# Feed-forward of a two-layer decoder trunk: a third column block by seven products in every second group, squares by ScalarE, first activations transposed by TensorE

## The chip, the core and the metric

The kernel runs on one core of a Trainium2 chip. A core has five engines with instruction streams of their own: TensorE (PE in the profile; its weight loads are PEld), VectorE (DVE), ScalarE (ACT), GpSimd (POOL) and SyncE (SP), which here only starts DMAs. Each takes its instructions in the order in which they stand and waits on semaphores. TensorE writes its products into PSUM, eight banks of 512 fp32 columns; the other engines copy them out. The metric is the device time of one execution, in microseconds, as the median of several runs.

## What is computed

Two layers, each a mixer and a dense feed-forward (FFN) with a squared ReLU. The change lies in the FFN, which runs once in each layer.

```python
# D_MODEL = 2048, SEQ = 256, DEPTH = 2, FFN_HIDDEN = 8192, all float32
def rmsnorm(x, w):
    y = x * lax.rsqrt(jnp.mean(jnp.square(x), axis=-1, keepdims=True) + EPS)
    return y * w

def squared_relu_mlp(h, w_up, w_down):
    return jnp.square(jax.nn.relu(h @ w_up)) @ w_down

def reference(x, ...):
    h = x                                   # (1, 256, 2048)
    for layer in range(DEPTH):              # 0: linear attention, 1: spatial gating
        y = mixer(rmsnorm(h, norm_w[layer, 0]), ...)
        h = h + rmsnorm(y, norm_w[layer, 1])
        y = squared_relu_mlp(rmsnorm(h, norm_w[layer, 2]), ffn_w_up[layer], ffn_w_down[layer])
        h = h + rmsnorm(y, norm_w[layer, 3])
    return h
```

## The kernel before

**Numbers.** Every fp32 product is made of three matmuls. `split` and `weights` divide an operand into a rounded part (hi, type fp32r, by ScalarE: lines 125 and 189) and the remainder (lo, by VectorE: lines 126 and 190); a product is x_hi·w_hi + x_lo·w_hi + x_hi·w_lo (lines 132 to 134, 318 to 320 and 362 to 364).

**Weights.** They come from HBM in tiles of 128 x 2048 fp32 (1 MB) over SP's queue into three buffers (`raw`), and are divided into four buffers of hi (`whi`) and four of lo (`wlo`). A buffer is used again when its last reader is done.

**The FFN.** `first_chunk` makes the first 512 of the 8192 hidden columns with tokens on the partitions (two halves of 128 tokens, b = 0 and 1). Its result must be turned round, hidden columns onto partitions: VectorE does that with 16 transposes of 32 x 32 blocks for each half (`blocks`, line 218). Then a loop runs over c = 1 to 15. A pass of it makes the next 512 hidden columns (`up_pass`, four quarters of 48 matmuls of 256 columns, PSUM tiles `tp`), and multiplies the 512 before them, group g = c - 1, with the down weights, in four blocks of 512 output columns (`block`), one behind each quarter: the order is `ORDER`, and in the first pass `FIRST`, where block 1 stands behind the second quarter, block 0 behind the third, and blocks 3 and 2 behind the fourth. `relu2` takes ReLU on ScalarE (line 386) and squares on GpSimd (line 387); the result is divided into the tiles e, and `sums` (lines 398 to 401) makes the sums f that seven-product blocks want. The last group is done by `down_last`, which also normalises.

**The blocks.** Blocks 0 and 2 (`SEVEN`) are made by seven products instead of eight: the 256 x 512 block is taken as 2 x 2 halves (Strassen's scheme in Winograd's form), `mul7` adds weights on VectorE (lines 341 to 343, tile `qsum`) and divides 1536 plain and 2048 summed columns, so that two `whi` and two `wlo` buffers are taken, and `chunk7` issues 42 matmuls of 256 columns into four PSUM tiles, two of the pool `acc` and two of `mx`, which VectorE adds to four accumulators (line 416). After the loop `combine` makes the two result tiles of a block from these (lines 441 to 447). Block 1 (`KEPT`) is made plainly by 24 matmuls of 512 columns that accumulate in two PSUM banks (`kept`) through all 15 groups; `acc_to_y` copies them after the last. Block 3 is made plainly, and copied or added to `y` in each group (lines 240 and 242). The pool `acc` has four banks, of which `kept` holds two; `mx` and `tp` have two each.

**Order.** The kernel is written in program order; a scheduler sets the order of each engine's instructions from it, with weight preparation and PSUM copies moved ahead or back, and that order is fixed when the program is built.

## Time and profile before

| | |
|---|---|
| median of three runs | 2547.78 us (2545.24 to 2547.9) |
| profiled execution: time / span | 2548.88 us / 2547.1 us |
| mean granted TensorE clock | 0.994 |
| TensorE, VectorE, ScalarE, GpSimd busy | 2506.0, 1968.8, 1201.2, 285.8 us |
| one pass in the middle of a FFN loop, from ReLU to ReLU | 43.69 us |
| in such a pass: TensorE, VectorE, ScalarE, GpSimd busy | 43.69, 37.00, 21.67, 2.58 us |
| GpSimd's squares (line 387) | 64, 83.0 us in all |
| VectorE's transposes of the first activations (line 218, from rl) | 64, 19.3 us in all |

The span runs from the first to the last instruction; the execution's time has 1.78 us around it. Busy shares are means over the program; matmuls are pipelined, so the time from the start of one to the start of the next says more than the duration that the profile gives to one. Idle time stands in brackets with the engine and line that ended it.

### The profile page before, as it was taken

To read this page: it belongs to the slowest core of one execution; us is meant where nothing else is said; L and a number is where in the kernel's file an instruction comes from. 1 tells how busy PE (TensorE), PEld (TensorE's weight loads), DVE (VectorE), ACT (ScalarE), POOL (GpSimd) and SP (SyncE) were. 2 spreads that over 40 slices of the span, in tenths; PEclk is the share of its full clock that TensorE was granted. 3 is DMA by queue.
4 is the path that set the end of the run, shared out by engine and by line. 5 is a ranking of instruction groups with operands and counts; after the bars stand their busy time and mean duration, and the time that the engine had idled before them with its cause. 6 is when DMAs were issued, how large, how long until landed. Compare 5 with 4: busy or idle time off the path is not lost.

```text
span 2547.1 us, 36465 instructions
## 1 busy us (share of the span) xinstructions
PE 2506.0 (98%) x15138; PEld 2211.3 (87%) x15138; DVE 1968.8 (77%) x2256; ACT 1201.2 (47%) x1174; POOL 285.8 (11%) x222
## 2 busy tenths in 40 slices
PE   8999999999999999999999999999999999999998
PEld 7778888878999999999878877777789999999997
DVE  7586855579888888888854596876898888888887
ACT  6555444454454454545544333333544544445453
POOL 3000201140000000000310110110400000000001
PEclk9999999999999999999999999999999999999999
DMA  6444544544555455555555455555445554555553
GB/s 245 181 151 147 187 162 175 204 155 174 195 195 199 183 204 192 190 192 205 204 204 194 170 203 202 190 202 199 149 165 199 189 206 185 198 192 189 191 201 139
DMA packets 81255, 478.04 MB, mean 188 GB/s; under 512 B 13633, under 2 KB 15809, under 8 KB 26817
## 3 DMA queue, kind: packets, MB, share of 16 engines
q1 hardware_dynamic: 81088, 475.70, 51.1%
q8 instruction: 119, 1.95, 0.3%
q14 instruction: 48, 0.39, 0.0%
HBM read 473.04 MB, written 2.62 MB: 187 GB/s over the span
## 4 chain that ended last, share of the span: by engine, by line
PE 45%; DVE 4%; POOL 1%; issue 1%; ACT 0%; DVEq 0%; POOLq 0%; ACTq 0%
PE acc L133 9%; PE acc L134 9%; PE acc L132 9%; PE tp L318 4%; PE tp L319 4%; PE tp L320 4%; PE acc L362 1%; PE acc L364 1%; PE acc L363 1%; DVE wlo L126 1%; PE mx L363 1%; PE mx L362 1%; PE mx L364 1%; DVE h L275 1%; DVE bc L218 1%
## 5 line engine op out<-in xcount | busy, mean ns | idle before, releaser
L126 DVE TENSOR_TENSOR wlo<-raw,whi 128x2048 fp32r<-128x2048 f32 (+3 forms) x380 | 860.3, 2267 | 269.1 <-ACT whi L125 267.1
L125 ACT ACTIVATE whi<-raw 128x2048 fp32r<-128x2048 f32 (+3 forms) x380 | 714.1, 1880 | 566.3 <-PE acc L133 319.2
L318 PE MATMUL tp<-xh,whi 128*128 128x256 f32 x1920 | 539.5, 281 | 0.0
L319 PE MATMUL tp<-xl,whi 128*128 128x256 f32 x1920 | 539.2, 281 | 0.0
L320 PE MATMUL tp<-xh,wlo 128*128 128x256 f32 x1920 | 538.9, 281 | 0.0
L132 PE MATMUL acc<-whi,xh 128*128 128x512 f32 (+3 forms) x1120 | 446.3, 398 | 5.8 <-ACT whi L125 5.8
L134 PE MATMUL acc<-wlo,xh 128*128 128x512 f32 (+3 forms) x1120 | 440.0, 393 | 5.1 <-DVE wlo L126 5.1
L133 PE MATMUL acc<-whi,xl 128*128 128x512 f32 (+3 forms) x1120 | 438.9, 392 | 0.0
L318 PEld LDWEIGHTS tp<-xh,whi 128*128 128x128 f32 x1920 | 361.5, 188 | 2.7
L319 PEld LDWEIGHTS tp<-xl,whi 128*128 128x128 f32 x1920 | 361.6, 188 | 2.5
L320 PEld LDWEIGHTS tp<-xh,wlo 128*128 128x128 f32 x1920 | 361.7, 188 | 0.0
L134 PEld LDWEIGHTS acc<-wlo,xh 128*128 128x128 f32 x1120 | 212.1, 189 | 53.2 <-DVE wlo L126 7.0
L132 PEld LDWEIGHTS acc<-whi,xh 128*128 128x128 f32 x1120 | 212.4, 190 | 51.8 <-ACT whi L125 6.3
L133 PEld LDWEIGHTS acc<-whi,xl 128*128 128x128 f32 x1120 | 212.3, 190 | 44.7 <-issue 1.0
L387 POOL TENSOR_TENSOR rl<-rl 128x512 f32<-128x512 f32 x64 | 83.0, 1313 | 1261.0 <-ACT rl L386 1136.3
L189 ACT ACTIVATE whi<-qsum 128x2048 fp32r<-128x2048 f32 x60 | 115.3, 1922 | 179.9 <-DVE qsum L343 178.9
L190 DVE TENSOR_TENSOR wlo<-qsum,whi 128x2048 fp32r<-128x2048 f32 x60 | 138.7, 2312 | 79.0 <-ACT whi L189 77.0
L416 DVE TENSOR_TENSOR y<-acc,y 128x512 f32<-128x512 f32 x112 | 76.9, 687 | 86.1 <-PE acc L364 86.1
L189 ACT ACTIVATE whi<-raw 128x1536 fp32r<-128x1536 f32 x60 | 89.6, 1493 | 108.2 <-DMA raw<-dn 79.0
L133 PE MATMUL acc<-whi,e1l 128*128 128x512 f32 x288 | 114.0, 396 | 0.0
L134 PE MATMUL acc<-wlo,e1h 128*128 128x512 f32 x288 | 113.8, 395 | 0.0
L132 PE MATMUL acc<-whi,e1h 128*128 128x512 f32 x288 | 113.7, 395 | 0.0
(350 smaller groups left out, 4212.8 us busy)
## 6 DMA issues: line engine op xcount, KB each, us to landing
raw<-up SPq DMA_DIRECT2D x128, 1024.0 KB, 4.8
raw<-dn SPq DMA_DIRECT2D x128, 1024.0 KB, 4.8
raw<-sg_in SPq DMA_DIRECT2D x64, 1024.0 KB, 4.8
raw<-la_in SPq DMA_DIRECT2D x56, 1024.0 KB, 4.8
raw<-sg_out SPq DMA_DIRECT2D x32, 1024.0 KB, 4.8
raw<-la_out SPq DMA_DIRECT2D x16, 1024.0 KB, 4.8
raw<-la_in SPq DMA_DIRECT2D x4, 768.0 KB, 4.4
kq<-xT SPq DMA_DIRECT2D x8, 256.0 KB, 6.1
```

The costliest lines, as they stand in the source:

```text
L125: ACT.activation(a, r, AF.Copy)
L126: V.tensor_tensor(d, r, a.bitcast(F32), ALU.subtract)
L132: PE.matmul(ps, xh, wh, start=first, stop=False)
L133: PE.matmul(ps, xl, wh, start=False, stop=False)
L134: PE.matmul(ps, xh, wl, start=False, stop=last)
L189: ACT.activation(hi, src, AF.Copy)
L190: V.tensor_tensor(lo, src, hi.bitcast(F32), ALU.subtract)
L318: PE.matmul(out, wh[:, col], xh, start=k == 0 and m % 2 == 0, stop=False, skip_group_check=True)
L319: PE.matmul(out, wh[:, col], xl, start=False, stop=False, skip_group_check=True)
L320: PE.matmul(out, wl[:, col], xh, start=False, stop=k == NKT - 1, skip_group_check=True)
L387: G.tensor_tensor(r, r, r, ALU.mult)
L416: V.tensor_tensor(Y[key], ps, Y[key], ALU.add)
```

## The change

Four things change, all in `ffn`; the line numbers of the mixers move by one.

1. `SEVEN` holds block 1 as well. In groups with an odd g (seven of the 15) block 1 goes through `chunk7` into accumulators of its own; in the eight with an even g it still accumulates in the two `kept` banks. These are no longer copied after the last group: `combine(1)` adds them from PSUM.
2. `relu2` squares on ScalarE (Square, in place) instead of GpSimd.
3. The first activations are transposed by TensorE, four transposes of 128 x 128 for each half into a PSUM tile of `mx`, which ScalarE copies to SBUF (tile `rl`). VectorE's 32 transposes of each FFN are gone.
4. The accumulators are allocated at the start of the FFN; two of the three of 256 columns share a tile.

```diff
--- before.py
+++ after.py
@@ -30,7 +30,7 @@
 PARTS = [4, 2, 1, 1]
 WAIT = [26, 30]
 AHEAD = 200
-SEVEN, KEPT = (0, 2), 1
+SEVEN, KEPT = (0, 1, 2), 1
 ORDER = (None, 0, None, 1, None, 2, None, 3)
 FIRST = (None, None, 1, None, 0, None, 3, 2)
 
@@ -384,7 +384,7 @@
             def relu2(ps):
                 r = T(fp, [P, 512], "rl", bufs=3)
                 ACT.activation(r, ps, AF.Relu)
-                G.tensor_tensor(r, r, r, ALU.mult)
+                ACT.activation(r, r, AF.Square)
                 return r
 
             def rows_in(tags):
@@ -408,28 +408,22 @@
 
             Y, kept = {}, [bank(acc, 512, "acc") for _ in range(2)]
 
-            def add(key, ps, first, n=512):
-                if first:
-                    Y[key] = T(hp, [P, 512], *BUF[key])[:, :n]
-                    V.tensor_copy(Y[key], ps)
-                else:
-                    V.tensor_tensor(Y[key], ps, Y[key], ALU.add)
-
-            BUF = {("a", 0): ("y00",), ("b", 0): ("y10",), ("a", 2): ("y02",), ("b", 2): ("y12",)}
+            half = T(hp, [P, 512], "bc", bufs=4)
+            Y.update({("d", 0): half[:, :256], ("d", 2): half[:, 256:], ("d", 1): T(fp, [P, 256], "d1")})
             for c in SEVEN:
-                BUF["c", c] = BUF["d", c] = ("bc", F32, 4)
+                Y["a", c], Y["b", c] = T(hp, [P, 512], f"y0{c}"), T(hp, [P, 512], f"y1{c}")
+                Y["c", c] = T(hp, [P, 512], "bc", bufs=4)
 
             def block(c, g, e, f):
 
-                if c in SEVEN:
-                    ps = chunk7(dn, fp, e, f, rows(g), c * 512)
-                    for k, p, n in zip("abcd", ps, (512, 512, 512, 256)):
-                        add((k, c), p, g == 0, n)
+                if c in SEVEN and not (c == KEPT and g % 2 == 0):
+                    for k, p in zip("abcd", chunk7(dn, fp, e, f, rows(g), c * 512)):
+                        if g == (c == KEPT):
+                            V.tensor_copy(Y[k, c], p)
+                        else:
+                            V.tensor_tensor(Y[k, c], p, Y[k, c], ALU.add)
                 elif c == KEPT:
                     chunk_tok(dn, kts([e]), rows(g), [(c * 512, 512)], 512, kept, g == 0, g == last - 1)
-                    if g == last - 1:
-                        for b in range(2):
-                            acc_to_y(kept[b], b, c, True)
                 else:
                     for b, p in enumerate(chunk_tok(dn, kts([e]), rows(g), [(c * 512, 512)], 512)):
                         acc_to_y(p, b, c, g == 0)
@@ -445,15 +439,22 @@
                 V.tensor_tensor(u, u, b[:, r], ALU.add)
                 V.tensor_tensor(b[:, l], u, p[:, r], ALU.add)
                 V.tensor_tensor(b[:, r], p[:, l], u, ALU.subtract)
+                if c == KEPT:
+                    V.tensor_tensor(a, kept[0], a, ALU.add)
+                    V.tensor_tensor(b, kept[1], b, ALU.add)
                 y[0][c], y[1][c] = a, b
 
             def halves_of(tiles):
                 return [[t[:, m] for m in range(2)] for t in tiles]
 
             e = pair("e0")
-            t = [T(hp, [P, 512], "bc", bufs=4) for _ in range(2)]
+            t = []
             for b, ps in first_chunk(up, X, [(0, 512)]):
-                blocks(t[b], relu2(ps))
+                r, tp = relu2(ps), bank(mxp, 512, "mx")
+                for j in range(4):
+                    PE.transpose(tp[:, j * P : (j + 1) * P], r[:, j * P : (j + 1) * P], ident)
+                t.append(T(fp, [P, 512], "rl", bufs=3))
+                ACT.activation(t[b], tp, AF.Copy)
                 sl = slice(b * P, (b + 1) * P)
                 split(e[0][:, :, sl], e[1][:, :, sl], t[b].rearrange("p (j c) -> p j c", c=P))
             v = [a.rearrange("p (i m t) -> p i m t", i=2, t=P) for a in t]
```

The scheduler moves other work with it. **First place: TensorE in the first pass, from block 3 to block 2** (`acc` of line 362 is block 2's first tile in PSUM, `mx` its others, `tp` the up products). Before, from the first product of block 2:

```order
L362 MATMUL mx_957_5179<-whi_952_5166,f0h_903_4787 128x256
L363 MATMUL mx_957_5179<-whi_952_5166,f0l_904_4788 128x256
L364 MATMUL mx_957_5179<-wlo_954_5168,f0h_903_4787 128x256
L362 MATMUL mx_957_5179<-whi_952_5166,f0h_903_4787 128x256
L363 MATMUL mx_957_5179<-whi_952_5166,f0l_904_4788 128x256
L364 MATMUL mx_957_5179<-wlo_954_5168,f0h_903_4787 128x256
L362 MATMUL mx_959_5181<-whi_953_5167,f0h_903_4787 128x256
L363 MATMUL mx_959_5181<-whi_953_5167,f0l_904_4788 128x256
L364 MATMUL mx_959_5181<-wlo_955_5169,f0h_903_4787 128x256
L362 MATMUL mx_959_5181<-whi_953_5167,f0h_903_4787 128x256
L362 MATMUL acc_956_5178<-whi_952_5166,e0h_882_4614 128x256
L363 MATMUL acc_956_5178<-whi_952_5166,e0l_883_4615 128x256
```

Changed, up to the first product of block 2 into `acc`:

```order
L363 MATMUL mx_968_5168<-whi_962_5154,e0l_894_4626 128x256
L364 MATMUL mx_968_5168<-wlo_964_5156,e0h_893_4625 128x256
L318 MATMUL tp_971_5217<-xh0_816_4336,whi_974_5220 128x256
L319 MATMUL tp_971_5217<-xl0_817_4337,whi_974_5220 128x256
L320 MATMUL tp_971_5217<-xh0_816_4336,wlo_975_5221 128x256
L318 MATMUL tp_971_5217<-xh0_816_4336,whi_974_5220 128x256
L319 MATMUL tp_971_5217<-xl0_817_4337,whi_974_5220 128x256
L320 MATMUL tp_971_5217<-xh0_816_4336,wlo_975_5221 128x256
L318 MATMUL tp_972_5218<-xh0_816_4336,whi_974_5220 128x256
L319 MATMUL tp_972_5218<-xl0_817_4337,whi_974_5220 128x256
L320 MATMUL tp_972_5218<-xh0_816_4336,wlo_975_5221 128x256
L362 MATMUL acc_965_5165<-whi_961_5153,e0h_893_4625 128x256
```

Ten products of block 2 into `mx` stood ahead of its first one into `acc`; now eighteen do, and nine up products of the next pass.

**Second place: VectorE in the same pass**, from the sums of the next pass's weights (line 341) to the copy of block 3 out of PSUM (line 240), by which block 2's first `acc` bank comes free. Before:

```order
L341 TENSOR_TENSOR qsum_972_5291<-raw_971_5290 128x1024
L400 TENSOR_TENSOR tr_940_5119<-rl_938_5109 128x256
L342 TENSOR_TENSOR qsum_972_5291<-qsum_972_5291,raw_971_5290 128x512
L343 TENSOR_TENSOR qsum_972_5291<-qsum_972_5291,raw_971_5290 128x512
L126 TENSOR_TENSOR wlo_970_5238<-raw_968_5236,whi_969_5237 128x2048
L190 TENSOR_TENSOR e1l_906_4792<-rl_938_5109,e1h_905_4791 128x512
L190 TENSOR_TENSOR e1l_906_4792<-rl_939_5112,e1h_905_4791 128x512
L398 TENSOR_TENSOR tr_940_5119<-rl_938_5109,rl_939_5112 128x256
L240 COPY y03_948_5160<-acc_943_5128 128x512
```

Changed:

```order
L341 TENSOR_TENSOR qsum_977_5274<-raw_976_5273 128x1024
L342 TENSOR_TENSOR qsum_977_5274<-qsum_977_5274,raw_976_5273 128x512
L400 TENSOR_TENSOR tr_949_5106<-rl_947_5096 128x256
L343 TENSOR_TENSOR qsum_977_5274<-qsum_977_5274,raw_976_5273 128x512
L190 TENSOR_TENSOR e1l_919_4783<-rl_947_5096,e1h_918_4782 128x512
L398 TENSOR_TENSOR tr_949_5106<-rl_947_5096,rl_948_5099 128x256
L399 TENSOR_TENSOR tr_949_5106<-tr_949_5106,rl_947_5096 128x256
L401 TENSOR_TENSOR tr_949_5106<-tr_949_5106,rl_948_5099 128x256
L126 TENSOR_TENSOR wlo_975_5221<-raw_973_5219,whi_974_5220 128x2048
L190 TENSOR_TENSOR e1l_919_4783<-rl_948_5099,e1h_918_4782 128x512
L190 TENSOR_TENSOR f1l_951_5112<-tr_949_5106,f1h_950_5111 128x1024
L240 COPY y03_957_5147<-acc_952_5115 128x512
```

The copy stood behind four instructions on the activations (400, 190, 190, 398) and now stands behind all seven, the division of the sums f among them.

**Third place: VectorE in an odd pass** (g = 3), around block 0's four additions to its accumulators (line 416 before, 424 changed; from two tiles `acc` and two `mx`). Before, where block 1 is plain, up to the sums of block 2's weights:

```order
L416 TENSOR_TENSOR y00_931_5047<-acc_1075_6166,y00_931_5047 128x512
L126 TENSOR_TENSOR wlo_1084_6272<-raw_1082_6270,whi_1083_6271 128x2048
L416 TENSOR_TENSOR y10_932_5049<-acc_1077_6168,y10_932_5049 128x512
L416 TENSOR_TENSOR bc_934_5053<-mx_1076_6167,bc_934_5053 128x256
L416 TENSOR_TENSOR bc_933_5051<-mx_1078_6169,bc_933_5051 128x512
L126 TENSOR_TENSOR wlo_1087_6302<-raw_1085_6300,whi_1086_6301 128x2048
L341 TENSOR_TENSOR qsum_1089_6355<-raw_1088_6354 128x1024
L190 TENSOR_TENSOR wlo_1092_6358<-raw_1088_6354,whi_1090_6356 128x1536
L342 TENSOR_TENSOR qsum_1089_6355<-qsum_1089_6355,raw_1088_6354 128x512
```

Changed, from the sums of block 1's weights to those of block 2's:

```order
L341 TENSOR_TENSOR qsum_1095_6288<-raw_1094_6287 128x1024
L342 TENSOR_TENSOR qsum_1095_6288<-qsum_1095_6288,raw_1094_6287 128x512
L424 TENSOR_TENSOR y00_884_4616<-acc_1087_6183,y00_884_4616 128x512
L424 TENSOR_TENSOR bc_882_4614<-mx_1088_6184,bc_882_4614 128x256
L343 TENSOR_TENSOR qsum_1095_6288<-qsum_1095_6288,raw_1094_6287 128x512
L424 TENSOR_TENSOR y10_885_4617<-acc_1089_6185,y10_885_4617 128x512
L190 TENSOR_TENSOR wlo_1098_6291<-raw_1094_6287,whi_1096_6289 128x1536
L424 TENSOR_TENSOR bc_886_4618<-mx_1090_6186,bc_886_4618 128x512
L190 TENSOR_TENSOR wlo_1099_6292<-qsum_1095_6288,whi_1097_6290 128x2048
L126 TENSOR_TENSOR wlo_1106_6353<-raw_1104_6351,whi_1105_6352 128x2048
L341 TENSOR_TENSOR qsum_1108_6406<-raw_1107_6405 128x1024
```

The weight sums and divisions of block 1 (341 to 343, and two of 190) now stand between and behind block 0's four additions; those of block 2 follow at once.

## Rows read from the trace of the kernel before

**Rows 1.** The page's busy times by engine (busy us, share of the span, instructions).

```profile
PE 2506.0 (98%) x15138; PEld 2211.3 (87%) x15138; DVE 1968.8 (77%) x2256; ACT 1201.2 (47%) x1174; POOL 285.8 (11%) x222
```

**Rows 2.** Who waited for whom on TensorE, whole program: waiting line, what it waited for, us in total, times, longest.

```profile
PE acc L362 <- DVE y L240: 9.0, 2, 4.5
...
PE mx L690 <- DVE PT L693: 3.4, 2, 2.2
...
PE acc L133 <- DVE e0l L190: 0.8, 2, 0.4
```

**Rows 3.** Instructions of TensorE in order of time, in one pass in the middle of the second FFN: the first matmul of an up quarter, of block 0 (seven products), of the next up quarter, of block 1 (plain), of the up quarter behind it. Columns: start, us, engine, line, operation, out<-in, shape, count.

```profile
1991.68 0.28 PE L318 MATMUL tp<-xh,whi 128*128 128x256 f32 x1
...
1997.36 0.28 PE L362 MATMUL acc<-whi,e1h 128*128 128x256 f32 x1
...
2002.26 0.28 PE L318 MATMUL tp<-xh,whi 128*128 128x256 f32 x1
...
2007.93 0.39 PE L132 MATMUL acc<-whi,e1h 128*128 128x512 f32 x1
...
2013.53 0.28 PE L318 MATMUL tp<-xh,whi 128*128 128x256 f32 x1
```

**Rows 4.** The same pass as a window: length, busy us of PE, PEld, DVE, ACT, POOL (instructions that start in it), granted clock, DMA share, GB/s.

```profile
1985.58:2029.27 43.69, 43.69 (x326) 41.49 (x325) 37.00 (x34) 21.67 (x15) 2.58 (x2) 1.00 0.55 195
```

**Rows 5.** Instructions in order of time, in the same pass: GpSimd's two squares (its only work there), and VectorE's.

```profile
1986.31 2.58 POOL L387 TENSOR_TENSOR rl<-rl 128x512 f32<-128x512 f32 x2 [41.12 <-ACT rl L386]
...
1986.45 1.53 DVE L342 TENSOR_TENSOR qsum<-qsum,raw 128x512 f32<-128x512 f32 x1
...
2006.04 1.22 DVE L341 TENSOR_TENSOR qsum<-raw 128x1024 f32<-128x1024 f32 x1
2007.17 1.75 DVE L190 TENSOR_TENSOR wlo<-raw,whi 128x1536 fp32r<-128x1536 f32 x1
2008.84 0.69 DVE L342 TENSOR_TENSOR qsum<-qsum,raw 128x512 f32<-128x512 f32 x1
2009.56 0.69 DVE L343 TENSOR_TENSOR qsum<-qsum,raw 128x512 f32<-128x512 f32 x1
2012.32 2.29 DVE L190 TENSOR_TENSOR wlo<-qsum,whi 128x2048 fp32r<-128x2048 f32 x1 [2.07 <-ACT whi L189]
...
2020.81 0.69 DVE L416 TENSOR_TENSOR y<-acc,y 128x512 f32<-128x512 f32 x1 [3.01 <-PE acc L364]
2021.41 2.28 DVE L126 TENSOR_TENSOR wlo<-raw,whi 128x2048 fp32r<-128x2048 f32 x1
...
2024.21 1.01 DVE L416 TENSOR_TENSOR bc<-mx,bc 128x256 f32<-128x256 f32 x2
```

**Rows 6.** Groups of instructions by line and shape, whole program (count, busy us, mean ns, idle before): GpSimd's squares, and squares that ScalarE makes elsewhere on a tile of the same size.

```profile
L387 POOL TENSOR_TENSOR rl<-rl 128x512 f32<-128x512 f32 x64 | 83.0, 1313 | 1261.0 <-ACT rl L386 1136.3 <-DVE rl L441 82.2 <-issue 42.5
...
L227 ACT ACTIVATE junk<-y 128x512 bf16<-128x512 f32 x32 | 20.0, 626 | 42.3 <-DVE y L263 42.3
```

**Rows 7.** TensorE in order of time, around block 2 of the first pass, in the first FFN (its first matmul into `mx`, and the first up matmul behind it), then in the second: the first matmul of block 1 and the first up matmul behind that; the first matmul of block 2 into `mx`, its first into `acc`, and the first up matmul behind it.

```profile
616.34 0.28 PE L362 MATMUL mx<-whi,f0h 128*128 128x256 f32 x1
...
628.29 0.28 PE L318 MATMUL tp<-xh,whi 128*128 128x256 f32 x1
...
1863.74 0.39 PE L132 MATMUL acc<-whi,e0h 128*128 128x512 f32 x1
...
1870.01 0.28 PE L318 MATMUL tp<-xh,whi 128*128 128x256 f32 x1
...
1891.86 0.28 PE L362 MATMUL mx<-whi,f0h 128*128 128x256 f32 x1
...
1897.66 0.58 PE L362 MATMUL acc<-whi,e0h 128*128 128x256 f32 x1 [4.48 <-DVE y L240]
...
1904.30 0.28 PE L318 MATMUL tp<-xh,whi 128*128 128x256 f32 x1
```

**Rows 8.** Windows (columns as in rows 4): after the wait of line 690 in the first mixer, and behind the wait of line 362 in the second FFN.

```profile
248.37:251.78 3.41, 3.25 (x8) 2.65 (x9) 1.75 (x7) 0.00 (x0) 0.00 (x0) 0.50 0.28 118
1897.01:1903.83 6.82, 6.17 (x29) 6.17 (x30) 5.91 (x8) 2.97 (x2) 0.00 (x0) 0.50 0.63 251
```

**Rows 9.** VectorE in order of time, from the start of the second FFN to the copy that the wait of line 362 is put down to.

```profile
1844.08 5.04 DVE L218 STREAM_TRANSPOSE bc<-rl 32x128 f32<-32x128 f32 x16 [0.92 <-POOL rl L387]
...
1857.23 5.03 DVE L218 STREAM_TRANSPOSE bc<-rl 32x128 f32<-32x128 f32 x16
...
1896.93 0.68 DVE L240 COPY y<-acc 128x512 f32<-128x512 f32 x1
```

**Rows 10.** TensorE in order of time, ahead of the second FFN: four transposes of 128 x 128 between matmuls of 512 columns.

```profile
1841.15 0.66 PE L207 MATMUL tp<-ident,e 128*128 128x128 f32 x4
1841.56 0.48 PE L134 MATMUL acc<-wlo,xh 128*128 128x512 f32 x1
1841.88 0.39 PE L132 MATMUL acc<-whi,xh 128*128 128x512 f32 x1
```

**Rows 11.** The end of the second FFN: TensorE's first matmul of `down_last`, and VectorE's additions of block 3 and the first three additions of `down_last`.

```profile
2516.00 0.39 PE L132 MATMUL acc<-whi,e1h 128*128 128x512 f32 x1
...
2516.94 1.28 DVE L242 TENSOR_TENSOR y<-acc,y 128x512 f32<-128x512 f32 x2
...
2524.70 1.89 DVE L263 TENSOR_TENSOR y<-acc,y 128x512 f32<-128x512 f32 x3
```

## Prediction

> **What bounds the kernel now.** The page's busy times come first: TensorE 98%, VectorE 77% [rows 1]. Then who TensorE waited for: the largest item is 9.0 us in two waits of 4.5, at line 362 for a copy of line 240 [rows 2]. Then one pass of the FFN loop in order of time and as a window: TensorE is busy 43.69 of 43.69 us, VectorE 37.00, ScalarE 21.67 [rows 3, 4]. The reader is to see two regimes. In the passes TensorE's stream alone sets the time, and VectorE has 6.69 us without work. At the start of each FFN VectorE is behind: TensorE waits for it, and is at half its clock afterwards [rows 7, 8].
>
> **Seven products for block 1.** The starts in [rows 3] give each stage's length: plain block 1 takes 5.60 us (24 matmuls, 0.233 each), a block of seven products 4.90 (42 matmuls, 0.117 each), an up quarter 5.68. So each group that changes saves 0.70 us; seven groups in each of two FFNs make 14: **-9.8 us**.
>
> The Trainium skill, "TensorE: Matmul & The Clock Gate", section "Back-to-back issue gap", speaks against this: it gives a sustained 81 ns for a matmul of 128 columns and 131 ns for 512, so that half the width costs more than half the time; about 97 ns for 256 is my estimate between its figures, 4.1 us for 42 against 3.1 us for 24, a block dearer by 1 us. By that the sum would be 14 us worse than before instead of 9.8 better. [Rows 3] show 0.117 against 0.233, exactly half, and decide.
>
> VectorE pays for it. With durations taken from start to start in [rows 5], a block of seven products needs sums 1.13 + 0.72 + 0.6, divisions 1.67 + 2.2, and four additions, 3 x 0.6 + 0.35 (a half one): 8.5 us. A plain block 1 needs one division, 2.2. So an odd pass has 6.3 us more, against 43.69 - 0.70 = 42.99 us of TensorE. Squares on ScalarE give some back: beside GpSimd's squares the same instruction of line 342 took 1.53 instead of 0.69 [rows 5]; two such losses a pass are 1.7 us, an estimate. VectorE's odd pass is then 37.00 + 6.3 - 1.7 = 41.6 of 42.99. That fits, with 1.4 us to spare, if VectorE waits no more than that. Its waits are for TensorE (3.01 in the row) and for ScalarE's division of the sums (2.07) [rows 5]. I walked the new order through one odd pass with these durations: VectorE now comes to each addition after the product is done, so the waits for TensorE go; before the third seven-product block its weights' last part is ready 1.7 us before TensorE wants it, before the second 3.8 us. The even pass behind has 8 us to recover in. I take **0**; bounds are 0 and 0.5 us in each of 14 passes, 7 us, by the error of that walk.
>
> **Squares on ScalarE.** 64 of 1.31 us leave GpSimd, and 64 of about 0.63 come to ScalarE (its squares of that size elsewhere) [rows 6]. ScalarE's odd pass becomes 21.67 + 1.3 + at most 1.75 for the wider division (VectorE's own time for it [rows 5], an upper bound): 25 of 43 us. Queued behind the squares on ScalarE are the next weights' divisions, which wait for buffers most of the time; 18 us of idle cover it: **0**. Without that cover it is 1.3 us a pass.
>
> **Transposes by TensorE, at the start of each FFN.** From its first matmul to the next up matmul, block 2 of the first pass takes 628.29 - 616.34 = 11.95 us and 1904.30 - 1891.86 = 12.44 [rows 7] instead of 4.90: 14.6 us lost in both, by a wait of 4.48 each and by a granted clock of 0.50 (1.2 of 2.4 GHz) for 6.8 us [rows 7, 8]. Block 1 before it takes 1870.01 - 1863.74 = 6.27 instead of 5.60, waiting for e0l [rows 2, 7]; the other FFN has the same wait, so 1.3 us in both. VectorE's transposes, 5.04 + 5.03 us in each FFN, stand ahead of all of this [rows 9]; TensorE needs e at 1863.7, and without 10 us of VectorE's work it has it, so the 1.3 us go.
>
> Whether the 14.6 go depends on when line 240's copy ends. It began at 1896.93 [rows 9]. In its favour: no GpSimd squares beside VectorE, and part of the 10.1 us. Not all of these, since VectorE must still wait for block 0's products, which come no sooner. Against it: the copy now stands behind lines 399, 401 and the division of f (0.35 + 0.35 + 1.13, by columns from [rows 5]). But TensorE wants the bank later: 27 matmuls instead of 10 stand between block 3 and that product, 17 x 0.117 = 2.0 us. So the copy has to end by about 1895.3 instead of 1897.6. Walking VectorE's order from block 0's first product on gives 1895.0 to 1895.6. I take 0.5 us of wait left in each FFN, and that this is too short to bring the low clock: **-14.6 - 1.3 + 1.0**.
>
> The transposes themselves: four take 0.41 us from their start to the next matmul, and the one behind that comes 0.32 later instead of 0.233 [rows 10]: 0.5 for four, sixteen in all: **+2.0**; bounds 1.6 and 3.0. ScalarE copies them to SBUF at about 0.6 each beside idle time. TensorE would wait at the transposes if ReLU and square came late; they stand some 1.3 to 2.3 us behind the product, about what ScalarE needs, so a few tenths at most. The Trainium skill, same page, section "Part 4: PE-mode transpose", gives about 275 ns for one in a kernel; by that it is 4.4 us instead of 2.0, and the sum 2.4 us smaller. [Rows 10] have four within 0.66, and start the next matmul earlier still; they decide.
>
> **The end.** `down_last`'s first product began at 2516.00, right behind block 3, in a bank that `kept` had left [rows 11]. Now the `kept` banks are held until `combine(1)`, so it waits for VectorE to add block 3's first half. That began at 2516.94 and takes 0.6 [rows 11], 1.5 us too late by then; ReLU and square on ScalarE bring it forward by about 1 us. Behind it VectorE has `combine(1)` more, seven half steps of 0.35 and two of 0.6, 3.6 us, before it divides the last weights and frees banks (first at 2524.70 before [rows 11]), with about 2 us of room. I take 0.9 us in each FFN, **+1.8**; bounds 0.3 and 3.
>
> **The sum**: -9.8 - 14.6 - 1.3 + 1.0 + 2.0 + 1.8 = **-20.9 us**. The profiled execution's span of 2547.1 becomes 2526.2, its time of 2548.88 becomes 2528.0. It was 1.1 us above the median of 2547.78, so I forecast **2526.9 us**.
>
> **Rivals.**
> *The start stays late.* VectorE comes to the copy no earlier than before, since it waits for other things in place of the transposes (weights from HBM, block 0). For it: the copy is behind more instructions. Against it: 10 us less ahead. Then 4.48 - 2.0 = 2.5 us of wait stay, and a low clock: a wait of 2.2 us in the mixer [rows 2] was followed by 3.4 us at 0.50 [rows 8], 1.7 us lost. 4.2 instead of 0.5 in each FFN: 2526.9 + 7.4 = 2534 us. The same time comes out if each odd pass is 0.5 us late.
>
> *VectorE can't keep up in odd passes; slower.* Three seven-product blocks follow each other, and VectorE, in order, keeps the waits that it has now, 43.69 - 37.00 = 6.69 us a pass [rows 4], above all for ScalarE's division of the sums, where only 1.4 fit. Each odd pass is then late by up to 5.3 us: 14 x 5.3 = 74, 2601 us. It decides from 1.5 us of lateness a pass on, which eat the 20.9. For it: 41.6 of 42.99 is 97% of an engine that takes its work in order. Against it: the walk, and half the waits are for TensorE, which a late engine doesn't have.
>
> *Narrow products cost more than half a wide one.* If a matmul could not start sooner after another than the mean busy time of a load, 2211.3 us over 15138 or 0.146 [rows 1], 42 would take 6.1 us against 5.6, and the gain of 9.8 would be a loss of 7.5: 2544 us. (The skill's issue-gap section, above, points this way.) [Rows 3] have it at 0.117 already; 1%.
>
> **Chances.** The forecast with its bounds, 2521 to 2532: 0.58. Late start or slightly late odd passes, 2532 to 2542: 0.22. Gains all eaten, within 0.2% (5 us, about what a measurement of this kernel can tell from no change): 0.07, the narrow products among them. Slower: 0.10. Better than 2521: 0.03. So faster 0.83, same 0.07, slower 0.10. The range of 8 in 10 takes in the first two: 2520 to 2542. The sum without any of the costs that I added is -25.7, 2522 us, so little lies below it.
>
> **What will show it.** Odd passes of 43.0 us and even ones of 43.7, TensorE without a wait; VectorE busy about 41.6 us in the odd ones and 37.00 - 1.7 = 35.3 in the even. No wait at line 362 over 1 us, and block 2 of the first passes without a low clock. Line 342 near 0.7 us on the mean. TensorE's transposes about 0.1 us apart. `down_last` beginning within 1 us behind block 3. The prediction is wrong if odd passes are above 43.7, if TensorE waits there for wlo of lines 126 or 190, or if the wait for line 240's copy stays over 2 us.

## The result and the profile after

The changed kernel takes 2528.15 us (median of four runs, 2526.76 to 2528.85) against 2547.84 for the kernel before, on the same chip: 0.9926 of its time, 95% interval 0.9911 to 0.9941. The profiled execution has a span of 2527.0 us at a mean granted clock of 0.998. Forecast were 2526.9 us, between 2520 and 2542.

Three views answer to [rows 1, 2, 4]. The page's busy times:

```profile
PE 2490.6 (99%) x15406; PEld 2210.5 (87%) x15406; DVE 1991.3 (79%) x2318; ACT 1249.8 (49%) x1256; POOL 203.6 (8%) x158
```

Who waited for whom on TensorE:

```profile
PE acc L134 <- DVE wlo L126: 6.8, 5, 2.1
PE acc L132 <- ACT whi L125: 5.8, 1, 5.8
PE mx L691 <- DVE PT L694: 3.4, 2, 2.2
PE acc L132 <- DVE y L242: 2.8, 3, 1.2
```

An odd pass (its block 1 by seven products), the even pass behind it, and the first passes of both FFNs, as windows from ReLU to ReLU (columns as in rows 4):

```profile
1969.13:2012.12 42.99, 42.99 (x344) 41.89 (x343) 40.48 (x41) 23.74 (x18) 0.00 (x0) 1.00 0.53 192
2012.13:2055.82 43.69, 43.69 (x326) 41.49 (x325) 36.40 (x35) 22.59 (x17) 0.00 (x0) 1.00 0.56 197
...
1877.31:1925.43 48.12, 48.12 (x386) 46.93 (x385) 47.57 (x48) 27.04 (x20) 0.00 (x0) 1.00 0.53 189
610.31:658.43 48.12, 48.12 (x386) 46.93 (x385) 47.57 (x48) 27.04 (x20) 0.00 (x0) 1.00 0.52 188
```

The wait of line 362 is gone from the list, and the first passes, 55.66 and 56.13 us before, are at full clock without an idle moment. (The first stretch from ReLU to ReLU begins with blocks 3 and 2 of the first group, the later ones with block 3; so "first pass" holds the late block 2, and also the first block 1 by seven products.) The odd pass is 0.70 us shorter, the even one as before. The two timelines below answer to [rows 7, 9]: TensorE's first product of block 2 into `mx`, the first into `acc`, the next up product; and VectorE's copy of line 240.

```profile
1883.41 0.28 PE L362 MATMUL mx<-whi,f0h 128*128 128x256 f32 x1
...
1886.63 0.39 PE L362 MATMUL acc<-whi,e0h 128*128 128x256 f32 x1
...
1889.57 0.28 PE L318 MATMUL tp<-xh,whi 128*128 128x256 f32 x1
```

```profile
1885.89 1.28 DVE L240 COPY y<-acc 128x512 f32<-128x512 f32 x2
```

The copy begins 8.6 us behind the pass's ReLU (1877.31); before it was 11.2 (1896.93 against 1885.75). The first half of the copy ends as TensorE comes to the bank.

Where the span's 20.1 us went, by landmarks that both traces have (the first and last ReLU of each loop, a wait of TensorE in each mixer):

| stretch | before | after | difference |
|---|---|---|---|
| start to the mixer's wait at line 690 (691) | 248.53 | 247.47 | -1.06 |
| on to the first ReLU of the first loop | 361.71 | 362.84 | +1.13 |
| first FFN, first to last ReLU | 623.68 | 611.94 | -11.74 |
| on to a wait of line 132 in the second mixer | 555.03 | 557.61 | +2.58 |
| on to the first ReLU of the second loop | 96.80 | 97.45 | +0.65 |
| second FFN, first to last ReLU | 624.14 | 611.94 | -12.20 |
| on to the end | 37.21 | 37.75 | +0.54 |

The first row is code that doesn't change and begins differently from run to run.

### The profile page after: what moved, and what is told of

It is laid out like the page before. It is cut to its first block, busy times and chain, and to the rows that moved or that the text cites. A ratio compares the mean times of both kernels' runs of the same rounds, so it can differ in the third digit from the quotient of the medians.

```text
span 2527.0 us, 37082 instructions
## 1 busy us (share of the span) xinstructions
PE 2490.6 (99%) x15406; PEld 2210.5 (87%) x15406; DVE 1991.3 (79%) x2318; ACT 1249.8 (49%) x1256; POOL 203.6 (8%) x158
## 4 chain that ended last, share of the span: by engine, by line
PE 46%; DVE 3%; POOL 1%; issue 0%; ACT 0%; DVEq 0%; POOLq 0%; ACTq 0%
PE acc L134 8%; PE acc L132 8%; PE acc L133 8%; PE tp L318 4%; PE tp L320 4%; PE tp L319 4%; PE acc L362 1%; PE acc L363 1%; PE acc L364 1%; PE mx L362 1%; PE mx L363 1%; PE mx L364 1%; DVE h L275 1%; DVE wlo L126 1%; PE mx L1059 1%
## 5 line engine op out<-in xcount | busy, mean ns | idle before, releaser
L126 DVE TENSOR_TENSOR wlo<-raw,whi 128x2048 fp32r<-128x2048 f32 (+3 forms) x366 | 828.9, 2267 | 275.1 <-ACT whi L125 273.3
L125 ACT ACTIVATE whi<-raw 128x2048 fp32r<-128x2048 f32 (+3 forms) x366 | 687.1, 1878 | 490.6 <-PE acc L133 313.0
L189 ACT ACTIVATE whi<-qsum 128x2048 fp32r<-128x2048 f32 x74 | 142.1, 1920 | 211.4 <-DVE qsum L343 202.1
L190 DVE TENSOR_TENSOR wlo<-qsum,whi 128x2048 fp32r<-128x2048 f32 x74 | 169.5, 2290 | 66.7 <-ACT whi L189 66.7
L189 ACT ACTIVATE whi<-raw 128x1536 fp32r<-128x1536 f32 x74 | 110.5, 1493 | 183.5 <-DMA raw<-dn 73.3
L424 DVE TENSOR_TENSOR y<-acc,y 128x512 f32<-128x512 f32 x136 | 92.3, 686 | 49.7 <-PE acc L364 49.4
L190 DVE TENSOR_TENSOR wlo<-raw,whi 128x1536 fp32r<-128x1536 f32 x74 | 129.7, 1753 | 0.4
L265 POOL TENSOR_TENSOR e0h<-y,f1h 128x512 f32<-128x512 f32 x8 | 13.0, 1648 | 1349.9 <-DVE y L263 1349.9
L133 PE MATMUL acc<-whi,e0l 128*128 128x512 f32 x256 | 101.2, 395 | 0.0
L134 PE MATMUL acc<-wlo,e0h 128*128 128x512 f32 x256 | 101.1, 395 | 0.0
```

Source lines behind the costliest of these rows:

```text
L125: ACT.activation(a, r, AF.Copy)
L126: V.tensor_tensor(d, r, a.bitcast(F32), ALU.subtract)
L133: PE.matmul(ps, xl, wh, start=False, stop=False)
L134: PE.matmul(ps, xh, wl, start=False, stop=last)
L189: ACT.activation(hi, src, AF.Copy)
L190: V.tensor_tensor(lo, src, hi.bitcast(F32), ALU.subtract)
```

## Experiments

Twelve kernels ran, each timed against the kernel before on the same chip; the table has six of them, the text the others. The kernel before took 2546.6 to 2547.8 us on these chips, so the times of two kernels from different chips can differ by about 1 us for that alone. "Pass" is ReLU to ReLU in the trace: the first pass (both FFNs where they differ), then odd and even.

| kernel | time, us | against before | first pass | odd / even pass |
|---|---|---|---|---|
| before | 2547.8 | | 55.7, 56.1 | 43.69 |
| changed | 2528.2 | -19.7 | 48.1 | 42.99 / 43.69 |
| seven products alone | 2585.9 | +39.2 | 54.9, 54.2 | 45.45 / 44.80 |
| transposes alone | 2541.6 | -5.1 | 50.4 | 43.69 |
| squares alone | 2539.7 | -7.0 | 51.4 | 43.69 |
| changed, VectorE transposes | 2533.7 | -13.0 | 50.8, 52.3 | 42.99 / 43.69 |
| changed, GpSimd squares | 2582.3 | +35.2 | 49.7 | 45.45 / 44.82 |
| seven products always | 2515.9 | -30.8 | 48.0 | 42.99 |

### The parts alone, and taken away

Seven products alone is the changed kernel with these lines (and the other transposes) put back:

```diff
-                ACT.activation(r, r, AF.Square)
+                G.tensor_tensor(r, r, r, ALU.mult)
...
-                r, tp = relu2(ps), bank(mxp, 512, "mx")
-                for j in range(4):
-                    PE.transpose(tp[:, j * P : (j + 1) * P], r[:, j * P : (j + 1) * P], ident)
-                t.append(T(fp, [P, 512], "rl", bufs=3))
-                ACT.activation(t[b], tp, AF.Copy)
+                blocks(t[b], relu2(ps))
```

> The kernel before with the seven products of block 1 in odd groups alone (and the accumulators that they need): GpSimd squares, VectorE transposes the first activations. What the prediction says: 14 blocks at 0.70 us less, 9.8 us, and some 1.8 us more at the two ends; the starts keep what they lose (4.48 us of wait at line 362 and 6.8 us of low clock in each FFN), so about 2540 us, if VectorE keeps up: it has 37.00 + 6.3 = 43.3 us in an odd pass of 42.99, and can only make that up in the even pass behind it (37.00 of 43.69). Rival: an engine that works in order cannot shift work into the next pass, and GpSimd's squares have to go first: then each odd pass is late by 0.3 us at least and by up to 5, and the time is 2545 us or more.

It is slower than the kernel before, 1.0153 (1.0136 to 1.0170): each pair of passes 3.56 us late. The rival is right, and the prediction's own rival on VectorE with it: without the other two parts the third block costs more than it saves.

Transposes alone is the third part of the change in the kernel before; squares alone is its second part.

> The kernel before with the TensorE transposes of the first activations alone. The prediction puts the stall at the start of each FFN down to VectorE being late, 10 us of it by its own transposes: without these the copy of line 240 comes early enough, or nearly. Here the squares stay on GpSimd, and ten products stand between block 3 and block 2's first one into acc, not 27, so a wait of up to 2.5 us may stay; block 2 of the first pass 5 to 8 us instead of 12, the time 2535 to 2543 us. Rival: VectorE is held up there by other things (block 0's products, weights), and the changed kernel lost the stall because of the 27 matmuls and the squares: then the wait stays near 4.5 us and the time near 2547.

> The kernel before with the squares on ScalarE alone. The order of TensorE around block 2 of the first pass is then that of the changed kernel (27 matmuls ahead of the first product into acc, 9 of them up products). If VectorE's transposes make the stall, 2.0 us of it go by that order and about 1 by the squares: a wait of 1.5 to 2.5 us stays at line 362 in each FFN, with a low clock behind it or without, and the time is 2537 to 2544 us. Rival: order and squares alone take it away: no wait over 0.5 us, and 2533 to 2535 us, as much as the changed kernel gains at the starts. In the passes nothing changes but VectorE's busy time, 37.0 to 35.3 us.

0.9978 (0.9968 to 0.9987) and 0.9973 (0.9961 to 0.9985). TensorE's waits at the start, with the transposes alone and then with the squares alone:

```profile
PE acc L362 <- DVE y L240: 3.2, 2, 1.6
PE mx L458 <- POOL rl L387: 2.7, 4, 0.9
```

```profile
PE acc L362 <- DVE y L240: 2.5, 2, 1.2
PE tp L320 <- DVE wlo L126: 2.1, 2, 1.1
```

Each part cuts the 4.48 us to less than half, and in both traces no low clock follows. The first passes lose 11.1 us in sum by the transposes and 8.9 by the squares, 14.1 by both: they overlap. So the transposes are not the one cause, though the prediction put the whole term under their heading; with the squares alone 1.24 us stay at line 362, where 1.5 to 2.5 were expected, but 1.0 to 1.1 us appear at line 320 ahead of it. The transposes alone also make TensorE wait 0.9 us for GpSimd's square of the second half.

With VectorE's transposes put back into the changed kernel:

> The changed kernel with VectorE's transposes of the first activations put back (into two tiles of their own): seven products and ScalarE squares stay, and so does the order of the changed kernel around block 2 of the first pass. If VectorE's transposes are the main part of the stall, the wait at line 362 comes back as 2.0 to 2.5 us in each FFN (4.48 less the 2.0 of the order), perhaps with a low clock, e0l waits again, the TensorE transposes' 1 to 2 us go: 2532 to 2537 us. By the run with the squares alone, where the first pass was 51.4 us (47.97 of work, 2.3 of waits, the rest of pitch), it is 50.7 against 48.12: 5 us worse at the two starts and some 2 us better without the transposes, 2531 us. Rival: the order and the squares suffice, no wait, about 2526.

2533.7 us, 5.5 above the changed kernel. Both FFNs have the same two waits, 1.06 to 1.13 us at line 320 and 1.24 at line 362. Windows over them, from 8.3 us behind the ReLU on (columns as in rows 4), differ in the granted clock; until it falls VectorE does the same work in both, and the lower counts in the second come behind the fall:

```profile
619.00:626.00 7.00, 4.62 (x37) 4.21 (x36) 6.76 (x9) 3.28 (x3) 0.00 (x0) 1.00 0.38 150
1888.00:1895.00 7.00, 4.69 (x26) 4.28 (x25) 5.58 (x8) 2.19 (x3) 0.00 (x0) 0.77 0.41 152
```

That is 50.8 against 52.3 us for the pass: waits of this size bring the low clock in one place and not in the other.

With GpSimd's squares put back into the changed kernel:

> The changed kernel with the squares back on GpSimd, and nothing else undone. A product on GpSimd beside the same order cost 11.6 us, later squares alone 8 us, none of it by odd passes. If the loss of the run with the seven products alone comes from contention, late squares and the order planned for them together, the passes are as in that run, 3.56 us late in each pair (some 43 us in all), the first passes some 1.6 us longer each, and TensorE's transposes wait 0.9 us twice for GpSimd: about 2575 us. Rival: that run was late because VectorE, 10 us behind from its transposes at the start, never caught up; without these the passes are 43.0 and 43.7, or 44.2 by contention: 2530 to 2542 us.

1.0136 (1.0119 to 1.0152). In this place ScalarE's squares are worth 54 us, for which the prediction had 0.

### What makes a pass late

What GpSimd's squares do was then taken apart: a product on GpSimd beside the unchanged order; squares that are late but made by ScalarE; more work for VectorE.

```diff
                 ACT.activation(r, r, AF.Square)
+                G.tensor_tensor(T(fp, [P, 512], "idle", bufs=2), r, r, ALU.mult)
```

> The changed kernel with a product on GpSimd behind each square, of the same size and kind as the squares that GpSimd made before; nothing reads its result, and VectorE's and TensorE's order is that of the changed kernel. It separates contention from lateness in the run with the seven products alone, which was 3.56 us late in each pair of passes. If contention makes that (GpSimd slows VectorE by some 1.5 us a pass), the odd pass's 1.4 us to spare are gone: odd passes late by 0.3 us or more, 2533 to 2560. If it is that the squares come late and VectorE, in order, waits for them (and the order planned from that), nothing is lost: VectorE's busy time in the odd pass goes from 40.5 to 42 of 42.99, with no wait on TensorE: 2526 to 2530 us.

2539.7 us, 11.6 above the changed kernel. Odd passes stay at 42.99 us, even ones become 44.16 (12 waits for line 190's f0l, 3.0 us in all, and products stretched beside them), and first passes and ends lose the rest. Lines 342 and 343 take 0.82 us on the mean instead of 0.69. TensorE, VectorE and ScalarE have the same instructions in the same order as in the changed kernel, and nothing waits for the added product. So contention is real; in this order it costs 11.6 us, about a fifth of the 54.

```diff
+                ACT.activation(r, r, AF.Copy)
                 ACT.activation(r, r, AF.Square)
```

> The changed kernel with a copy in place on ScalarE (about 0.6 us) between each ReLU and its square: the squares come later, by 0.6 us the first and 1.2 the second, as they did from GpSimd, but nothing slows VectorE; the order is planned anew from that, as it was for the run with the seven products alone. If lateness and that order made the 3.56 us in a pair of passes, a good part of it comes back here: 2535 to 2575 us. If contention made it, odd passes stay 43.0 and even ones 43.7: 2527 to 2531 us.

2536.2 us, but with odd passes of 42.99 and even ones of 43.69: the 8 us are lost in the first passes (50.2) and at the ends. Squares that are 0.6 to 1.2 us late make no odd or even pass late by themselves.

```diff
+MORE = 2
...
+        for _ in range(MORE if col == 512 else 0):
+            V.tensor_tensor(Q[:, 0:2, :], B[:, 1:3, :], B[:, 0:1, :].to_broadcast([P, 2, 512]), ALU.add)
         V.tensor_tensor(Q[:, 2, :], Q[:, 0, :], B[:, 2, :], ALU.add)
```

> The changed kernel with line 341 for block 1's weights made three times instead of once (the same values are written again): 2 x 1.22 us more on VectorE in each odd pass. VectorE's busy time: 40.48 + 2.44 = 42.92 of 42.99 in the odd pass, 39.7 on the mean of both. If busy time on the mean decides, as the run with seven products in every group suggests (41.3 us on the mean, no wait), nothing is lost: 2528 us. Rival: what decides is the room of one instruction, the division of the sums for block 2, which ends 1.9 us before TensorE's first product that wants it; 2.44 us ahead of it make each odd pass 0.5 us late, 14 x 0.5 = 7 us: 2535 us or above.

2574.1 us; odd passes 45.4, even 43.9, with VectorE busy for only 41.3 us of the odd one. Busy time doesn't decide. The rival's direction is right, its place and size (0.5 us in each odd pass, where 2.4 were lost) aren't: TensorE's largest wait in the pass (1.06 us) is for the up weights, which ScalarE divides only behind the sums' division, for which it waits for VectorE (L126 is L125, L346 is L343 here). ScalarE in order of time:

```profile
2030.05 1.92 ACT L190 ACTIVATE whi<-qsum 128x2048 fp32r<-128x2048 f32 x1 [7.72 <-DVE qsum L346]
2031.88 5.50 ACT L126 ACTIVATE whi<-raw 128x2048 fp32r<-128x2048 f32 x3
```

The sums pass from VectorE (lines 341 to 343) to ScalarE (hi) and back to VectorE (lo, line 190), and all engines take their work in order. In the kernel with GpSimd's squares VectorE's odd pass shows what that does; its order has nothing between the last sum and the division in the second and third block of seven products:

```profile
2017.63 0.69 DVE L343 TENSOR_TENSOR qsum<-qsum,raw 128x512 f32<-128x512 f32 x1
2020.38 2.29 DVE L190 TENSOR_TENSOR wlo<-qsum,whi 128x2048 fp32r<-128x2048 f32 x1 [2.07 <-ACT whi L189]
...
2030.32 0.69 DVE L343 TENSOR_TENSOR qsum<-qsum,raw 128x512 f32<-128x512 f32 x1
2033.08 2.29 DVE L190 TENSOR_TENSOR wlo<-qsum,whi 128x2048 fp32r<-128x2048 f32 x1 [2.07 <-ACT whi L189]
```

and TensorE, at the product that wants the second of these:

```profile
2035.43 0.38 PE L364 MATMUL acc<-wlo,f1h 128*128 128x256 f32 x1 [1.70 <-DVE wlo L190]
```

The changed kernel has work in the first of the two places (the two middle rows), and 1.9 us of room behind the second (the division is done at 2002.5, where the next starts; TensorE's product that wants it is at 2004.40):

```profile
1983.91 0.68 DVE L343 TENSOR_TENSOR qsum<-qsum,raw 128x512 f32<-128x512 f32 x1
1984.62 0.69 DVE L424 TENSOR_TENSOR y<-acc,y 128x512 f32<-128x512 f32 x1
1985.23 1.75 DVE L190 TENSOR_TENSOR wlo<-raw,whi 128x1536 fp32r<-128x1536 f32 x1
...
1987.49 2.29 DVE L190 TENSOR_TENSOR wlo<-qsum,whi 128x2048 fp32r<-128x2048 f32 x1
...
2000.30 2.29 DVE L190 TENSOR_TENSOR wlo<-qsum,whi 128x2048 fp32r<-128x2048 f32 x1 [2.07 <-ACT whi L189]
2002.52 2.28 DVE L126 TENSOR_TENSOR wlo<-raw,whi 128x2048 fp32r<-128x2048 f32 x1
```

```profile
2004.40 0.28 PE L364 MATMUL acc<-wlo,f1h 128*128 128x256 f32 x1
```

So the planner's order, which changes with the squares' engine, may be the cause. To test it, GpSimd's squares stay and the sums get a higher priority (lines 341 to 343, indented below it):

```diff
+        with tc.high_priority(offset=60):
```

> The changed kernel with the squares on GpSimd, as in the run before, but with the three sums of lines 341 to 343 at a higher priority for the planner. In the order that it makes, VectorE has 1.0 to 3.2 us of other work between the last sum and the division of the sums in all three seven-product blocks of an odd pass; in the run before it had 1.05 us in the first and nothing in the second and third, and waited 2.07 us for ScalarE there, twice. If these uncovered waits made the 3.56 us in each pair of passes, they go: passes of 43.0 and 43.7 or 44.2 (contention), about 2540 us (2532 to 2548). Rival: GpSimd's squares make the loss by being late and slowing VectorE, in whatever order: 2570 us or more.

2538.1 us, 44 below the same squares in the other order. Windows of an odd and an even pass, first in that other order, then in this one:

```profile
1998.18:2043.62 45.44, 43.74 (x346) 42.34 (x345) 40.61 (x40) 21.09 (x16) 2.57 (x2) 1.00 0.45 164
2043.62:2088.44 44.82, 43.78 (x324) 41.27 (x323) 38.49 (x36) 22.56 (x16) 3.10 (x2) 1.00 0.57 210
```

```profile
1977.04:2020.03 42.99, 42.99 (x344) 41.89 (x343) 40.81 (x40) 22.92 (x16) 2.72 (x2) 1.00 0.54 196
2020.04:2063.73 43.69, 43.69 (x326) 41.49 (x325) 38.15 (x36) 21.53 (x15) 3.83 (x2) 1.00 0.53 193
```

VectorE and GpSimd are as busy in both, and one is 3.58 us late in the pair, the other not at all. It is the order. The opposite test, ScalarE's squares and an order with the two places uncovered:

```diff
-        split(hi[0][:, :1536], lo[0][:, :1536], raw[:, 512:])
         split(hi[1], lo[1], q)
+        split(hi[0][:, :1536], lo[0][:, :1536], raw[:, 512:])
```

> The changed kernel (squares on ScalarE) with two lines exchanged: the sums' division is written ahead of that of the plain columns. In the order that the planner then makes, nothing stands between last sum and division in the second and third seven-product block of an odd pass, as in the run with GpSimd's squares; in the changed kernel only the third is so. If uncovered waits make the loss, odd passes are late by 1 to 3 us without any work of GpSimd: 2545 to 2575 us. Rival: without GpSimd beside VectorE there is no loss: 2527 to 2532 us.

2563.5 us, odd passes 44.90 without any GpSimd work: order alone can do it. But this isn't quite the same loss. TensorE's one wait in the odd pass is 1.43 us, for ScalarE's hi of the plain columns, which now stands behind the sums' division. The changed kernel leaves the second place uncovered and loses nothing by it; no run uncovers the first alone and changes nothing else, so what that one costs by itself stays open. ScalarE in order of time, then TensorE's list of waits:

```profile
2017.87 1.92 ACT L189 ACTIVATE whi<-qsum 128x2048 fp32r<-128x2048 f32 x1 [7.93 <-DVE qsum L343]
2019.69 1.47 ACT L189 ACTIVATE whi<-raw 128x1536 fp32r<-128x1536 f32 x1
```

```profile
PE acc L362 <- ACT whi L189: 20.5, 17, 1.4
```

### Seven products in every group

```diff
-                if c in SEVEN and not (c == KEPT and g % 2 == 0):
+                if c in SEVEN:
```

(and `kept`, its branch and its two additions are gone).

> The changed kernel with block 1 by seven products in every group: no banks are kept. VectorE has 38.44 us in the mean of an odd and an even pass now; with 6.3 more in each even one 41.6 of 42.99 in all. If busy time alone decides whether VectorE keeps up, 16 more blocks save 0.70 us each, 11.2 us, and the end loses its wait (2 to 3 us in both), since the banks are free: about 2515 us. Rival: an odd pass fits only because the even one behind it has 7 us of room; without it VectorE's waits (6.7 us a pass before, most for ScalarE's division of the sums) don't fit in 1.4 us, and each pass is late by 1 us or more: 2535 us and above.

2515.9 us, 0.9879 of before (0.9865 to 0.9894), and 11 to 12 us better than the changed kernel. Two passes behind each other:

```profile
1959.76:2002.75 42.99, 42.99 (x344) 41.89 (x343) 42.16 (x43) 23.86 (x19) 0.00 (x0) 1.00 0.57 201
2002.76:2045.75 42.99, 42.99 (x344) 41.90 (x343) 40.48 (x41) 23.72 (x19) 0.00 (x0) 1.00 0.52 192
```

VectorE is at 98% in one of them and nothing is late. VectorE's total wait at line 190 for ScalarE tells the kernels apart as its busy time does not; before, changed, GpSimd's squares in both orders, and this one, a line from each list of VectorE's waits (total, times, longest; the kernel before has 60 divisions of sums, the changed one 74, this one 90):

```profile
DVE wlo L190 <- ACT whi L189: 77.8, 58, 2.1
```

```profile
DVE wlo L190 <- ACT whi L189: 66.7, 54, 2.1
```

```profile
DVE wlo L190 <- ACT whi L189: 100.5, 69, 2.6
```

```profile
DVE wlo L190 <- ACT whi L189: 51.2, 42, 2.6
```

```profile
DVE wlo L190 <- ACT whi L189: 41.8, 43, 2.1
```

In the four kernels whose pairs of passes are more than 2 us late it is 93.8 to 101.0 us (more VectorE work 93.8, seven products alone 99.1, GpSimd's squares 100.5, the uncovered order 101.0); in all others it is 80.0 or less.

### The end

```diff
+                    if g == last - 1:
+                        for b in range(2):
+                            out = T(fp, [P, 512], f"k{b}")
+                            ACT.activation(out, kept[b], AF.Copy)
+                            kept[b] = out
```

> The changed kernel with the two banks of block 1 copied to SBUF by ScalarE (0.6 us each, beside 19 us of idle) right behind their last product, and read from there when the results are put together. If the held banks make the wait ahead of the last group's products (1.22 and 0.42 us before the first one), it goes in both FFNs: 1.6 us less by the span of these stretches. VectorE's work behind it stays, so the later waits at the transposes of line 207 (about 1.2 us more than before at the first end) stay or grow. 2526 to 2528 us. Rival: these waits are VectorE's own lateness, and move behind the last products: nothing gained between the last ReLU and the first transposes.

2528.8 us, no gain. From the last ReLU on, the first FFN's end is 1.6 us longer than in the changed kernel, the second's as long (37.71 against 37.74). The wait ahead of `down_last` is gone; in the first FFN the first and the last of these waits of TensorE are new, and the one between (0.83 in the changed kernel) has stayed:

```profile
1234.21 0.50 PE L134 MATMUL acc<-wlo,e1h 128*128 128x512 f32 x1 [0.83 <-DVE wlo L126]
1245.13 0.63 PE L207 MATMUL tp<-ident,e0h 128*128 128x128 f32 x4 [0.88 <-DVE e0h L279]
...
1264.49 0.50 PE L134 MATMUL acc<-wlo,xh 128*128 128x512 f32 x1 [0.76 <-DVE wlo L126]
```

The rival holds for this order: with the banks free VectorE is late all the same. In the kernel with seven products always, where no bank is held and `combine(1)` has two additions less, the ends cost 1.5 and 0.3 us more than before, against 2.6 and 0.5 in the changed kernel; what of that is the banks and what the shorter work isn't separated.

## Why the prediction was right, step by step

**Seven products, -9.8.** Right to the digit: six odd passes of each loop at 42.99 and one inside the first stretch, 14 times 0.70. By the estimate that the prediction worked out from the Trainium skill, "TensorE: Matmul & The Clock Gate", section "Back-to-back issue gap", these blocks would have been dearer. The trace does not agree: 42 matmuls of 256 columns take 4.90 us, as before.

**VectorE keeps up, 0.** Right, and the walk was good: the second block was to have 3.8 us of room and the third 1.7; they have 4.0 (the division done at 1989.8, the product that wants it at 1993.8) and 1.9. The busy time of a pair of passes, forecast 41.6 + 35.3, is 40.48 + 36.40: 76.9 in both. But the reason given ahead of the walk, 41.6 of 42.99, is no reason. With GpSimd's squares a pair was 3.6 us late at 79.1 of 86.68 us; with seven products always a pass of 42.16 in 42.99 was not late. The rival with the 6.69 us of waits had the mechanism (ScalarE's division of the sums), and it decided for slower as soon as the order left two divisions uncovered.

**Squares on ScalarE, 0.** This step failed as an account, though the sum didn't suffer: their relief was in VectorE's term, as 1.7 us a pass of contention, and the cost of missing cover as 1.3 us. Without them the change is 35 us slower than before instead of 20 faster. What they bring is mostly another order from the planner; with a covered order GpSimd's squares cost 10 us, not 54.

**The start, -14.6 + 1.0.** -14.1 measured. The sizes fit, the copy's end included (9.25 to 9.85 us behind the ReLU forecast, 9.2 by the rows). The weight on VectorE's transposes doesn't: transposes or squares alone each take most of it, the squares with the later place of block 2's `acc` products. With waits of 2.3 us (squares alone) or 1.6 us (transposes alone) in a first pass and no fall of the clock, 9 or 11 of the 14 us are already back.

**e0l and the transposes, -1.3 + 2.0 = +0.7.** +1.13 and +0.65, 1.8 us. e0l's wait went. Four transposes and the matmul behind them cost 0.41 and 0.32 as forecast; left out was the step into them, 0.38 and 0.33 instead of 0.23 and 0.12, as here in the second FFN:

```profile
1834.15 0.39 PE L132 MATMUL acc<-whi,xh 128*128 128x512 f32 x1
1834.53 0.66 PE L455 MATMUL mx<-ident,rl 128*128 128x128 f32 x4
1834.95 0.48 PE L133 MATMUL acc<-whi,xl 128*128 128x512 f32 x1
1835.26 0.39 PE L134 MATMUL acc<-wlo,xh 128*128 128x512 f32 x1
```

So some 0.68 for four instead of 0.5, 2.7 us for sixteen, inside the bounds of 1.6 and 3.0. Another 0.5 us of the +1.13 is not theirs: in the first mixer, which doesn't change, TensorE waited longer for a DMA (before, then changed):

```profile
PE mx L806 <- DMA y<-du: 0.2, 1, 0.2
```

```profile
PE mx L807 <- DMA y<-du: 0.7, 1, 0.7
```

**The end, +1.8.** Too small: +2.58 and +0.54, 3.1. The wait ahead of `down_last` was 1.22 and 0.42 us of idle (0.9 forecast for each):

```profile
1229.74 0.47 PE L132 MATMUL acc<-whi,e1h 128*128 128x512 f32 x1 [1.22 <-DVE y L242]
...
1246.92 0.63 PE L207 MATMUL tp<-ident,e0h 128*128 128x128 f32 x4 [0.83 <-DVE e0h L279]
```

The second row is what was missed: the first FFN's end runs into the next mixer's transposes, which the normalisation feeds. This wait was 0.42 before, and all waits at these transposes together are 3.2 us instead of 2.0: that costs some 1.2 us. So "about 2 us of room" for the longer `combine` did not hold.

In all, the span is 0.8 us above the 2526.2 forecast: the ends cost 1.3 us more than put down and the stretches ahead of the loops 1.1 (0.6 by the transposes, 0.5 by that wait for a DMA), the stalls gave 0.5 more back, and the unchanged start of the program was 1.06 us shorter in this execution. So the nearness of the forecast is in part luck: its terms were 1.4 us too small together, and code that doesn't change took 0.6 us less in this execution. The median is 1.25 above the forecast, since the profiled execution stood 1.1 us over its median before and 0.7 now (2528.85 against 2528.15).

## What to carry to other kernels

In these kernels an engine that works in order was late by the waits that stood uncovered in its queue, not by its busy share: where a value goes from VectorE to ScalarE and back, look at what VectorE does in between, and compare this place in the orders before and after. Moving a small operation to another engine can change the planner's order of everything behind it, so cost it by the order that comes out. When several parts of a change aim at one stall, each alone may remove most of it, and their gains don't add.

## What was not expected of the hardware

The low clock does not follow from the length of a wait alone: after waits of 1.06 to 1.13 and 1.24 us it fell to 0.50 for 3.41 us in one FFN and stayed at 1.00 in the other, and after 4.47 us in both (seven products alone) it was 0.50 for 6.83 us in one and for 3.41 in the other. GpSimd's product of 128 x 512 beside VectorE lengthened lines 342 and 343 by 0.13 us on the mean and cost 11.6 us where nothing else in any queue had moved. That mean hides two cases: the 32 of these instructions that ran beside GpSimd's product took 1.31 us on the mean, the 116 others 0.68. Why VectorE is slower beside it was not measured.
